# Splitting the weights of each quantum one quantum earlier, across job borders, in a hybrid mLSTM / gated delta rule block

## The chip, the cores and the metric

The kernel runs on one core of a Trainium2 chip. The metric is the device time of one launch in microseconds; for the kernel before, three runs took 1992.89, 1995.98 and 1995.86 us, with a median of 1995.86.

Five engines with an instruction queue each appear below: PE (TensorE, the matrix products), DVE (VectorE, elementwise work from SBUF), ACT (ScalarE, elementwise functions), POOL (GpSimd) and SP (which here issues the loads of weights). PEld is PE's weight load.

## The reference

One layer on 256 tokens of width 2048, in f32, cut to the parts that matter here:

```python
mod = silu(c) @ ada_w + ada_b                 # shift/scale/gate, twice
h = rms_norm(x) * (1 + scale_m) + shift_m
a_q, a_k, a_v, a_o, gates, b_qkv, b_z, gates, merge = split(h @ w_in)
qkv = silu(depthwise_conv5(b_qkv))            # 16 heads of 128: q, k, v
o_b = gated_delta_rule(qkv), both directions  # chunks of 64
h_a = mlstm(a_q, a_k, a_v), both directions   # 4 heads
y_a = (sigmoid(a_o) * rms_norm(h_a)) @ w_branch_a
y_b = (rms_norm(o_b) * silu(b_z)) @ w_branch_b
x = x + gate_m * ((g_a * y_a + g_b * y_b) @ w_out)   # g = sigmoid(merge)
gt, up = split(hf @ w_gate_up)                # hf = modulated rms_norm(x)
x = x + gate_f * ((silu(gt) * up) @ w_down)
out = rms_norm(x)
```

Nearly all the time goes into products of 256 rows with large weight matrices.

## The kernel before

**Products in three parts.** Each f32 weight is split into a high part (`wh`, the value rounded to the fast f32 format of PE) and a low part (`wl`, the rest), and the activations likewise (`hh` and `hl`). A product is the sum of three: high by high, low by high, high by low. The copy to `wh` runs on ACT and the subtraction to `wl` on DVE; both read a 1 MB tile `raw` that SP has loaded from HBM.

**Jobs and quanta.** A *job* is a generator that makes one block of output columns and yields after each *quantum*. `fjob` (L173) makes 128 features by 256 tokens from one raw tile, in 2 quanta of 24 products of 256 columns (L187 to L189). It is used for the heads of the gated delta rule (`b4_0` is head 4, q) and for mLSTM's q and k (`a0_3`). `tjob` (L199) makes 256 tokens by 512 features from four raw tiles or more, in 2 quanta per tile of 12 products of 512 columns (L234 to L236). It is used for v, o, z, the merge gates ma and mb, the branch projections ya and yb, the output projection (also called o, `o_job`), and the FFN's gt, up and d. At the start of a quantum, the halves of its raw tile are split: `fjob` at L182 and L184, `tjob` in `halves` (L207) at L213 and L215. Some t jobs (z0, o0, o3, gt0 and d3) are called with `early` or `by_token`: they split a fixed number of quanta ahead, with some of their instructions in written order.

**Buffers.** `raw`, `wh` and `wl` are tags of one pool with three buffers each, shared by all jobs; a new tile of a tag waits until the oldest one has been read for the last time. Until late in the kernel the tiles of the adaLN product (`ada`) use the `raw` tag as well. That product is done by the DVE, 64 tiles in all, and `raw_tile` (L136), `pump` and `add` spread it between the jobs.

**Order.** The program is a list in Python's order, which a scheduler uses as priority: it may let a ready instruction of an engine pass one that waits, except for those that `order` keeps in program order. `fills` is a list of jobs for which nothing waits soon, and `fill(n)` (L269) runs n quanta of its first job: v0 to v3, mb0, o0, a0_3, ma0, mb1, o1, a1_0 and so on. `stream(h0)` (L879) runs the six b jobs of two heads, then fills; between the quanta the caller places pieces of the recurrences (`gdn_phase1`, `gdn_phase2`). So a job in `fills` may be stopped in the middle and go on after a stream. `invert(g)` runs the DVE's inversion for four heads among fills, after `z_job(g)` was put in front of the fills (L1052). `y_bs` (L1110) runs the four yb jobs, as a fill of the mLSTM part.

**What is put off.** `settle` (L146) runs steps kept in `behind`, such as the SiLU that ends a convolution (L341, `vf`). Each split calls it between the copy and the subtraction.

The jobs start as follows in the profiled execution (us): z0 138, v0 to v3 161 to 234, mb0 259, o0 279, a0_3 300, ma0 306, b4 317, b5 336, b6 375, b7 394, mb1 417, z1 433, o1 466, a1 487, b8 496, b9 518, b10 564, b11 586, ma1 613, z2 624, mb2 662, o2 684, b12 690, b13 709, b14 750, b15 769, a2 800, z3 812, ma2 850, mb3 871, o3 897, a3 927, ma3 958, yb0 996, ya0 1101, gt0 1279, d0 1750. The first 140 us are the adaLN products on PE and the first heads' projections, as their loads arrive.

Of the kernel before, what the change touches and what calls it, by code (L numbers as in the profile page):

```python
# [9 lines left out]
F32 = mybir.dt.float32  # L10
F32R = mybir.dt.float32r
AF = mybir.ActivationFunctionType
ALU = mybir.AluOpType
PSUM = bass.MemoryType.PSUM

P = 128
# [36 lines left out]
def hybrid_block(ctx: ExitStack, tc: tile.TileContext, xr, nfr, crow, pk_d, cst_d, ada2, ada4, win0, winb, wint, wba, wbb, wo, wgu, wd, out, dbg=None):  # L53
# [17 lines left out]
    def order(ins, yes=True):  # L71

        return tc.keep_in_program_order(ins) if yes else ins
# [62 lines left out]
    def raw_tile(shape, name):  # L136

        since[0] += 1
        if since[0] > 2 and asked and room[0][0] is st:
            add()  # L140
        return st.tile(shape, F32, tag="raw", bufs=3, name=name)
# [4 lines left out]
    def settle(keep=0, only=None):  # L146

        now = [f for f in behind if only is None or f.__name__ == only]
        for f in now[: len(now) - keep]:
            behind.remove(f)  # L150
            f()
# [13 lines left out]
    def pump():  # L165
# [3 lines left out]
        if owed[0] and not held[0]:  # L169
            owed[0] -= 1  # L170
            sums()

    def fjob(name, src, done):  # L173

        ps = acc_ps.tile([P, 512], F32, tag="acc", name=f"acc_{name}")
        o = ps[:, :T]
        raw = raw_tile([P, KB, P], f"raw_{name}")
        nc.sync.dma_start(raw, src)
        for k0 in range(0, KB, 8):
            wh = st.tile([P, 8, P], F32R, tag="wh", bufs=3, name=f"wh_{name}_{k0}")  # L180
            wl = st.tile([P, 8, P], F32R, tag="wl", bufs=3, name=f"wl_{name}_{k0}")
            S.activation(wh, raw[:, k0 : k0 + 8], AF.Copy)  # L182
            settle()
            V.tensor_tensor(wl, raw[:, k0 : k0 + 8], wh.bitcast(F32), ALU.subtract)  # L184
            for k in range(8):
                kk = k0 + k
                PE.matmul(o, wh[:, k], woven(hh[:, kk]), start=kk == 0, stop=False)  # L187
                PE.matmul(o, wh[:, k], woven(hl[:, kk]), start=False, stop=False)  # L188
                PE.matmul(o, wl[:, k], woven(hh[:, kk]), start=False, stop=kk == KB - 1)  # L189
            if k0:  # L190
                pump()
                done(o.rearrange("p (c h) -> p h c", h=2))
            yield True
# [3 lines left out]
        return a.rearrange("p (h c) -> p c h", h=n)  # L197

    def tjob(name, chunks, xh, xl, done, early=0, by_token=None, steps=1, parts=((0, slice(0, 512)), (1, slice(0, 512)))):  # L199

        raws = {}

        def halves(u, k0):  # L207
            if u not in raws:
                raws[u] = raw_tile([P, 4, 512], f"raw_{name}_{u}")
                nc.sync.dma_start(raws[u], chunks[u])  # L210
            wh = st.tile([P, 2, 512], F32R, tag="wh", bufs=3, name=f"wh_{name}_{u}_{k0}")
            wl = st.tile([P, 2, 512], F32R, tag="wl", bufs=3, name=f"wl_{name}_{u}_{k0}")
            order(S.activation(wh, raws[u][:, k0 : k0 + 2], AF.Copy), early)  # L213
            settle()
            order(V.tensor_tensor(wl, raws[u][:, k0 : k0 + 2], wh.bitcast(F32), ALU.subtract), early)  # L215
            return wh, wl

        todo = [(u, k0) for u in range(len(chunks)) for k0 in (0, 2)]
        made = []
        for i, q in enumerate(todo[:early]):  # L220
            made.append(halves(*q))
            if steps > 1 or i == early - 1:
                yield True
        ps = [acc_ps.tile([P, 512], F32, tag="acc", name=f"acc_{name}_{t}") for t in range(2)]
        last = 4 * len(chunks) - 1
        if by_token:
            todo = todo[:-2]
        for n, (u, k0) in enumerate(todo):
            wh, wl = made.pop(0) if made else halves(u, k0)
            for k in range(2):  # L230
                kk = 4 * u + k0 + k
                for t in range(2):
                    c = slice(t * P, (t + 1) * P)
                    order(PE.matmul(ps[t], xh[:, kk, c], woven(wh[:, k]), start=kk == 0, stop=False), early and steps > 1)  # L234
                    PE.matmul(ps[t], xl[:, kk, c], woven(wh[:, k]), start=False, stop=False)  # L235
                    PE.matmul(ps[t], xh[:, kk, c], woven(wl[:, k]), start=False, stop=kk == last)  # L236
            if k0:
                pump()
                if u == len(chunks) - 1:
                    done(ps)  # L240
            yield True
            if early and steps > 1:
                if n + early < len(todo):
                    made.append(halves(*todo[n + early]))
                yield True
        if by_token:
            w = [halves(len(chunks) - 1, k0) for k0 in (0, 2)]
            by_token()
            for i, (t, part) in enumerate(parts):
                if i > 1:  # L250
                    ps.append(acc_ps.tile([P, 512], F32, tag="acc", name=f"acc_{name}_{i}"))
                c = slice(t * P, (t + 1) * P)
                o = ps[i][:, : part.stop - part.start]
                for k in range(4):
                    kk = last - 3 + k
                    wh, wl = (woven(a[:, k % 2])[:, part.start // 2 : part.stop // 2] for a in w[k // 2])
                    PE.matmul(o, xh[:, kk, c], wh, start=i == 2 and not k, stop=False)
                    PE.matmul(o, xl[:, kk, c], wh, start=False, stop=False)
                    PE.matmul(o, xh[:, kk, c], wl, start=False, stop=kk == last)
                done(t, ps[i], part)  # L260
                yield True
# [7 lines left out]
    def fill(n=1):  # L269

        while n and fills:
            if next(fills[0], None):
                n -= 1
            else:
                fills.pop(0)
# [97 lines left out]
    def b_job(h, j):  # L373
        return fjob(f"b{h}_{j}", winb[3 * (h - GRP) + j], lambda ps: gdn_conv(h, j, ps))
# [504 lines left out]
    def stream(h0):  # L879

        todo = []

        def piece():

            for q in list(todo):
                q[0] -= 1
                if not q[0]:
                    todo.remove(q)
                    next(heads1[q[1]])

        for h in range(h0, min(h0 + 2, NH_B)):
            for j in range(3):
                for _ in b_job(h, j):
                    piece()
                    yield True
            todo += [[2, h], [4, h]]
        while todo:
            fill(1)
            piece()
            yield True  # L900
        while True:
            fill(1)
            yield True
# [204 lines left out]
            split(mgh[:, b : b + 2], mgl[:, b : b + 2], px.rearrange("p (e t) -> p e t", e=2))  # L1108

    def y_bs():  # L1110
        for g in range(4):
            yield from y_b(g)

    o4s = [o_load(g) for g in range(2)]
    every[0] = owed[0] = 0
# [111 lines left out]
    class Late:  # L1227


        def __init__(self, key):  # L1230
            self.key = key
# [319 lines left out]
```

## Time and profile before

| | |
|---|---|
| runs | 1992.89, 1995.98, 1995.86 us (median 1995.86) |
| profiled execution | 1994.6 us |
| its span | 1992.6 us |
| mean granted PE clock | 0.992 of full speed |
| busy: PE / DVE / ACT | 1943.2 / 1393.9 / 1023.7 us |
| copies L182 (b) and L213 (d): mean | 1056 and 1056 ns |
| subtraction L184 (b): mean | 1216 ns |
| adaLN operation L111: mean, count | 2284 ns, 64 |
| loads raw_b: issue to landing, 1 MB | 5.3 us, median |

A group's row gives line, engine, operation, output and inputs with shapes, and the count; then busy time and the mean duration of one in ns; then how long the engine was idle just before these instructions, and what ended most of that. A row of waits says which instruction's line waited for which: total us, times, longest. A row of a timeline gives start, duration, engine and line; a bracket holds the idle time before. Products overlap: a product of 256 columns lasts 0.28 us in such a row, but the next starts 0.11 us later.

### The profile page before, as it was taken

Reading aid. Unit: us, or ns where it says so; the run is one execution under the profiler, and the core shown is the slowest. Engines: PE = TensorE matmul, PEld = TensorE weight load, DVE = VectorE, ACT = ScalarE, POOL = GpSimd, SP = SyncE. Lnnn points to the kernel's source line nnn. Section 1 sums busy time; section 2 is a strip of 40 time slices with the busy share of each in tenths; the row PEclk is TensorE's granted clock in tenths of the full one; section 3 lists DMA queues with packets and bytes.
Section 4 is the critical chain, followed back from the end, with each engine's and each line's share of the span. In section 5 each row is a group of like instructions: output and inputs, shape, how many; then the busy total and the mean of one; then the engine's idle time right before and its main releaser. Section 6 shows DMA issues by size and latency. Waiting matters only on the chain.

```text
span 1992.6 us, 27027 instructions
## 1 busy us (share of the span) xinstructions
PE 1943.2 (98%) x10386; PEld 1700.4 (85%) x10386; DVE 1393.9 (70%) x2062; ACT 1023.7 (51%) x1541; POOL 116.8 (6%) x211
## 2 busy tenths in 40 slices
PE   8999999999999999999999999999999999999998
PEld 6878789988988899889787888888888888888886
DVE  5778887877878788867576778866666665555554
ACT  3136646765756577655544444554444444444443
POOL 0001210111001101010100000200000000000000
PEclk9999999999989999999999999999999999999999
DMA  9987676655666666587786888466676775555654
GB/s 400 420 336 232 181 245 242 203 183 207 215 197 226 235 235 228 197 283 271 248 300 234 355 298 325 170 252 234 243 263 232 245 262 195 206 199 202 209 195 145
DMA packets 78962, 485.64 MB, mean 244 GB/s; under 512 B 10585, under 2 KB 15969, under 8 KB 24433
## 3 DMA queue, kind: packets, MB, share of 16 engines
q1 hardware_dynamic: 63216, 450.69, 62.4%
q0 software_dynamic: 8160, 17.88, 4.2%
q10 hardware_dynamic: 7458, 15.36, 2.1%
q8 instruction: 81, 1.33, 0.3%
q14 instruction: 47, 0.39, 0.1%
HBM read 467.07 MB, written 16.82 MB: 243 GB/s over the span
## 4 chain that ended last, share of the span: by engine, by line
PE 72%; DVE 12%; DMA 10%; ACT 3%; issue 2%; POOL 0%; ACTq 0%; SPq 0%; DVEq 0%; POOLq 0%
PE acc_gt L234 4%; PE acc_gt L235 4%; PE acc_gt L236 4%; PE acc_up L236 4%; PE acc_up L234 4%; PE acc_up L235 4%; PE acc_d L236 4%; PE acc_d L234 4%; PE acc_d L235 4%; DMA ra<-ada 3%; PE acc_o L236 2%; PE acc_o L234 2%; PE acc_o L235 2%; DMA ada<-ada 2%; PE acc_ya L236 1%
## 5 line engine op out<-in xcount | busy, mean ns | idle before, releaser
L215 DVE TENSOR_TENSOR wl_d<-raw_d,wh_d 128x1024 fp32r<-128x1024 f32 x88 | 107.7, 1224 | 109.2 <-ACT wh_d L213 109.2
L215 DVE TENSOR_TENSOR wl_up<-raw_up,wh_up 128x1024 fp32r<-128x1024 f32 x88 | 107.6, 1224 | 99.9 <-ACT wh_up L213 99.9
L215 DVE TENSOR_TENSOR wl_gt<-raw_gt,wh_gt 128x1024 fp32r<-128x1024 f32 x88 | 108.5, 1233 | 80.0 <-ACT wh_gt L213 80.0
L187 PE MATMUL acc_b<-hh,wh_b 128*128 128x256 f32 x576 | 164.2, 285 | 0.0
L189 PE MATMUL acc_b<-hh,wl_b 128*128 128x256 f32 x576 | 160.2, 278 | 0.1
L188 PE MATMUL acc_b<-hl,wh_b 128*128 128x256 f32 x576 | 159.2, 276 | 0.0
L213 ACT ACTIVATE wh_d<-raw_d 128x1024 fp32r<-128x1024 f32 x88 | 92.9, 1056 | 128.0 <-PE acc_d L235 119.2
L111 DVE SCALAR_TENSOR_TENSOR ada<-ada,crow 128x2048 f32<-128x2048 f32 x64 | 146.2, 2284 | 12.7 <-DMA ada<-ada 12.5
L213 ACT ACTIVATE wh_gt<-raw_gt 128x1024 fp32r<-128x1024 f32 x88 | 92.9, 1056 | 118.6 <-PE acc_gt L235 71.0
L213 ACT ACTIVATE wh_up<-raw_up 128x1024 fp32r<-128x1024 f32 x88 | 92.8, 1055 | 108.1 <-PE acc_up L235 77.1
L234 PE MATMUL acc_gt<-wh_gt,hfh 128*128 128x512 f32 x352 | 135.4, 385 | 0.2 <-ACT hfh L1338 0.2
L235 PE MATMUL acc_gt<-wh_gt,hfl 128*128 128x512 f32 x352 | 134.8, 383 | 0.0
L236 PE MATMUL acc_gt<-wl_gt,hfh 128*128 128x512 f32 x352 | 133.7, 380 | 0.0
L234 PE MATMUL acc_up<-wh_up,hfh 128*128 128x512 f32 x352 | 133.4, 379 | 0.0
L235 PE MATMUL acc_up<-wh_up,hfl 128*128 128x512 f32 x352 | 133.4, 379 | 0.0
L236 PE MATMUL acc_up<-wl_up,hfh 128*128 128x512 f32 x352 | 133.4, 379 | 0.0
L234 PE MATMUL acc_d<-wh_d,ffh 128*128 128x512 f32 x344 | 130.9, 380 | 0.0
L235 PE MATMUL acc_d<-wh_d,ffl 128*128 128x512 f32 x344 | 130.9, 380 | 0.0
L236 PE MATMUL acc_d<-wl_d,ffh 128*128 128x512 f32 x344 | 130.4, 379 | 0.0
L561 PE MATMUL first<-x,raw 128*128 128x256 f32 x512 | 114.5, 382 | 6.9 <-ACT x L555 6.2
L561 PEld LDWEIGHTS first<-x,raw 128*128 128x128 f32 x512 | 96.0, 190 | 25.3 <-ACT x L555 11.8
L189 PEld LDWEIGHTS acc_b<-hh,wl_b 128*128 128x128 f32 x576 | 111.3, 193 | 1.2 <-DVE wl_b L184 1.1
(374 smaller groups left out, 5237.5 us busy)
## 6 DMA issues: line engine op xcount, KB each, us to landing
ada<-ada SPq DMA_DIRECT2D x64, 1024.0 KB, 5.0
raw_gt<-wgu SPq DMA_DIRECT2D x44, 1024.0 KB, 4.9
raw_up<-wgu SPq DMA_DIRECT2D x44, 1024.0 KB, 4.9
raw_d<-wd SPq DMA_DIRECT2D x44, 1024.0 KB, 4.8
raw_b<-winb SPq DMA_DIRECT2D x36, 1024.0 KB, 5.3
ra<-ada SPq DMA_DIRECT2D x32, 1025.0 KB, 15.7
raw<-win SPq DMA_DIRECT2D x16, 1024.0 KB, 14.5
raw_z<-wint SPq DMA_DIRECT2D x16, 1024.0 KB, 5.2
```

The source lines that it names most:

```text
L111: order(V.scalar_tensor_tensor(raw, raw, 1.0, row_c[:, :D], ALU.mult, ALU.mult, accum_out=mod[:, c : c + 1]), room[0][3] > 1)
L187: PE.matmul(o, wh[:, k], woven(hh[:, kk]), start=kk == 0, stop=False)
L188: PE.matmul(o, wh[:, k], woven(hl[:, kk]), start=False, stop=False)
L189: PE.matmul(o, wl[:, k], woven(hh[:, kk]), start=False, stop=kk == KB - 1)
L213: order(S.activation(wh, raws[u][:, k0 : k0 + 2], AF.Copy), early)
L215: order(V.tensor_tensor(wl, raws[u][:, k0 : k0 + 2], wh.bitcast(F32), ALU.subtract), early)
L234: order(PE.matmul(ps[t], xh[:, kk, c], woven(wh[:, k]), start=kk == 0, stop=False), early and steps > 1)
L235: PE.matmul(ps[t], xl[:, kk, c], woven(wh[:, k]), start=False, stop=False)
L236: PE.matmul(ps[t], xh[:, kk, c], woven(wl[:, k]), start=False, stop=kk == last)
L561: PE.matmul(first[o], raw[:, o], x[:, b], start=b == 0 and o % 2 == 0, stop=b == KB - 1 and o % 2 == 1)
```

## The change

A class `Job` wraps the generators. `prime()` runs a job up to a first `yield` that now stands behind its first split, so that a job's load, copy and subtraction come ahead of the products of whatever runs before. `near_end` primes the next job when the present one has a quantum left; it is called in `fill`, for the next fill, and in `stream`, for the next b job or, behind the last, the first fill. Within a job, `tquanta` makes the split of the next quantum ahead of the products of the present one, and `fquanta` makes its second split ahead of its first products. The `settle()` of a split moves ahead of its copy. `y_bs` primes the next yb job ahead of the present one's last quantum. Jobs with `early` or `by_token` stay as they were, and so do the numbers of buffers.

```diff
--- before.py
+++ after.py
@@ -170,18 +170,54 @@
             owed[0] -= 1
             sums()
 
+    class Job:
+
+
+        def __init__(self, gen, quanta):
+            self.gen, self.left, self.primed = gen, quanta, False
+
+        def prime(self):
+            if not self.primed:
+                self.primed = True
+                next(self.gen)
+
+        def __iter__(self):
+            return self
+
+        def __next__(self):
+            self.prime()
+            self.left -= 1
+            return next(self.gen)
+
+    def near_end(job, after):
+
+        if isinstance(job, Job) and job.left == 1 and isinstance(after, Job):
+            after.prime()
+
     def fjob(name, src, done):
-
+        return Job(fquanta(name, src, done), 2)
+
+    def fquanta(name, src, done):
+
+        raw = raw_tile([P, KB, P], f"raw_{name}")
+        nc.sync.dma_start(raw, src)
+
+        def halves(k0):
+            wh = st.tile([P, 8, P], F32R, tag="wh", bufs=3, name=f"wh_{name}_{k0}")
+            wl = st.tile([P, 8, P], F32R, tag="wl", bufs=3, name=f"wl_{name}_{k0}")
+            settle()
+            S.activation(wh, raw[:, k0 : k0 + 8], AF.Copy)
+            V.tensor_tensor(wl, raw[:, k0 : k0 + 8], wh.bitcast(F32), ALU.subtract)
+            return wh, wl
+
+        made = [halves(0)]
+        yield False
         ps = acc_ps.tile([P, 512], F32, tag="acc", name=f"acc_{name}")
         o = ps[:, :T]
-        raw = raw_tile([P, KB, P], f"raw_{name}")
-        nc.sync.dma_start(raw, src)
         for k0 in range(0, KB, 8):
-            wh = st.tile([P, 8, P], F32R, tag="wh", bufs=3, name=f"wh_{name}_{k0}")
-            wl = st.tile([P, 8, P], F32R, tag="wl", bufs=3, name=f"wl_{name}_{k0}")
-            S.activation(wh, raw[:, k0 : k0 + 8], AF.Copy)
-            settle()
-            V.tensor_tensor(wl, raw[:, k0 : k0 + 8], wh.bitcast(F32), ALU.subtract)
+            if not k0:
+                made.append(halves(8))
+            wh, wl = made.pop(0)
             for k in range(8):
                 kk = k0 + k
                 PE.matmul(o, wh[:, k], woven(hh[:, kk]), start=kk == 0, stop=False)
@@ -197,12 +233,17 @@
         return a.rearrange("p (h c) -> p c h", h=n)
 
     def tjob(name, chunks, xh, xl, done, early=0, by_token=None, steps=1, parts=((0, slice(0, 512)), (1, slice(0, 512)))):
+        gen = tquanta(name, chunks, xh, xl, done, early, by_token, steps, parts)
+        return gen if early or by_token else Job(gen, 2 * len(chunks))
+
+    def tquanta(name, chunks, xh, xl, done, early, by_token, steps, parts):
 
 
 
 
 
         raws = {}
+        ahead = not (early or by_token)
 
         def halves(u, k0):
             if u not in raws:
@@ -210,8 +251,11 @@
                 nc.sync.dma_start(raws[u], chunks[u])
             wh = st.tile([P, 2, 512], F32R, tag="wh", bufs=3, name=f"wh_{name}_{u}_{k0}")
             wl = st.tile([P, 2, 512], F32R, tag="wl", bufs=3, name=f"wl_{name}_{u}_{k0}")
+            if ahead:
+                settle()
             order(S.activation(wh, raws[u][:, k0 : k0 + 2], AF.Copy), early)
-            settle()
+            if not ahead:
+                settle()
             order(V.tensor_tensor(wl, raws[u][:, k0 : k0 + 2], wh.bitcast(F32), ALU.subtract), early)
             return wh, wl
 
@@ -221,11 +265,16 @@
             made.append(halves(*q))
             if steps > 1 or i == early - 1:
                 yield True
+        if ahead:
+            made.append(halves(*todo[0]))
+            yield False
         ps = [acc_ps.tile([P, 512], F32, tag="acc", name=f"acc_{name}_{t}") for t in range(2)]
         last = 4 * len(chunks) - 1
         if by_token:
             todo = todo[:-2]
         for n, (u, k0) in enumerate(todo):
+            if ahead and n + 1 < len(todo):
+                made.append(halves(*todo[n + 1]))
             wh, wl = made.pop(0) if made else halves(u, k0)
             for k in range(2):
                 kk = 4 * u + k0 + k
@@ -269,6 +318,7 @@
     def fill(n=1):
 
         while n and fills:
+            near_end(fills[0], fills[1] if len(fills) > 1 else None)
             if next(fills[0], None):
                 n -= 1
             else:
@@ -888,12 +938,16 @@
                     todo.remove(q)
                     next(heads1[q[1]])
 
-        for h in range(h0, min(h0 + 2, NH_B)):
-            for j in range(3):
-                for _ in b_job(h, j):
-                    piece()
-                    yield True
-            todo += [[2, h], [4, h]]
+        jobs = [(h, j, b_job(h, j)) for h in range(h0, min(h0 + 2, NH_B)) for j in range(3)]
+        while jobs:
+            h, j, job = jobs.pop(0)
+            while job.left:
+                near_end(job, jobs[0][2] if jobs else fills[0] if fills else None)
+                next(job)
+                piece()
+                yield True
+            if j == 2:
+                todo += [[2, h], [4, h]]
         while todo:
             fill(1)
             piece()
@@ -1108,8 +1162,14 @@
             split(mgh[:, b : b + 2], mgl[:, b : b + 2], px.rearrange("p (e t) -> p e t", e=2))
 
     def y_bs():
+        after = y_b(0)
         for g in range(4):
-            yield from y_b(g)
+            job, after = after, None
+            while job.left:
+                if job.left == 1 and g < 3:
+                    after = y_b(g + 1)
+                    after.prime()
+                yield next(job)
 
     o4s = [o_load(g) for g in range(2)]
     every[0] = owed[0] = 0
```

## The prediction

> **What bounds the kernel now.** I read first the page's shares and its chain, then the busy time by stretches, then what TensorE (PE) waited for.
>
> ```profile
> span 1992.6 us, 27027 instructions
> PE 1943.2 (98%) x10386; PEld 1700.4 (85%) x10386; DVE 1393.9 (70%) x2062; ACT 1023.7 (51%) x1541; POOL 116.8 (6%) x211
> ...
> PE 72%; DVE 12%; DMA 10%; ACT 3%; issue 2%; POOL 0%; ACTq 0%; SPq 0%; DVEq 0%; POOLq 0%
> ```
>
> PE is busy 1943.2 of 1992.6 us, so whatever a reordering can win lies in 49 us. By stretches (columns: us, busy time of PE, weight load, VectorE (DVE), ScalarE (ACT) and POOL with counts, granted clock, DMA share, GB/s):
>
> ```profile
> 142.00:310.00 168.00, 163.92 (x783) 139.62 (x782) 138.19 (x279) 104.71 (x158) 29.57 (x55) 1.00 0.71 226
> 310.00:425.00 115.00, 113.67 (x887) 107.49 (x886) 92.71 (x174) 85.88 (x175) 10.43 (x21) 1.00 0.62 203
> 425.00:490.00 65.00, 63.49 (x308) 54.48 (x307) 51.96 (x112) 33.13 (x44) 9.94 (x19) 1.00 0.63 209
> 490.00:612.00 122.00, 114.89 (x943) 110.89 (x942) 95.19 (x177) 80.75 (x165) 9.91 (x20) 0.96 0.62 205
> 612.00:690.00 78.00, 74.29 (x349) 62.37 (x349) 62.25 (x128) 45.65 (x67) 10.48 (x20) 1.00 0.69 234
> 690.00:812.00 122.00, 116.05 (x914) 108.72 (x914) 101.98 (x205) 86.59 (x177) 10.34 (x21) 1.00 0.67 225
> 812.00:892.00 80.00, 78.15 (x443) 69.85 (x444) 62.06 (x108) 44.49 (x64) 12.64 (x23) 1.00 0.70 244
> ...
> 1290.00:1992.60 702.60, 692.76 (x3240) 601.50 (x3238) 402.48 (x395) 314.91 (x344) 0.50 (x1) 0.99 0.62 220
> ```
>
> 310–425, 490–612 and 690–812 hold the streams b4–b7, b8–b11 and b12–b15. PE idles 1.3, 7.1 and 6.0 us there, and in 490–612 it also ran below full clock. From 142 to 892 it idles 25.5 us in all. What it waited for (us in total, times, longest):
>
> ```profile
> PE vps L605 <- ACT vf L341: 6.3, 8, 3.1
> ...
> PE acc_mb L236 <- DVE wl_mb L215: 3.1, 3, 1.5
> PE acc_z L234 <- ACT wh_z L213: 2.5, 1, 2.5
> PE acc_z L236 <- DVE wl_z L215: 2.4, 3, 1.5
> PE acc_v L236 <- DVE wl_v L215: 2.4, 3, 1.4
> PE acc_ma L236 <- DVE wl_ma L215: 2.1, 1, 2.1
> PE p L762 <- DVE pt L754: 1.9, 1, 1.9
> PE p L787 <- DVE pt L776: 1.7, 1, 1.7
> ...
> PE acc_o L236 <- DVE wl_o L215: 0.8, 2, 0.5
> ```
>
> The waits on a split (wh, wl) make 13.3 us. That is the most the change's plain meaning, an earlier split, can win; and no product of the b jobs, the ones most rewritten, stands in these rows.
>
> **The change part by part.** Nothing is added or removed: the counts of products, copies, subtractions and DMAs are equal on every engine. About 225 PE, 194 ACT, 276 DVE instructions and 59 of SP's DMA issues stand elsewhere in the order, POOL's none, nearly all between 142 and 892 us. gt, up and d (1290 to the end) keep their order: 0 us.
>
> *1. When a split can start.* It needs a free wh and wl, of which there are three for all jobs together. In the streams the copy already starts on the release:
>
> ```profile
> 378.04 0.28 PE L188 MATMUL acc_b<-hl,wh_b 128*128 128x256 f32 x1
> ...
> 378.25 1.06 ACT L182 ACTIVATE wh_b<-raw_b 128x1024 fp32r<-128x1024 f32 x1
> ...
> 379.63 2.26 DVE L111 SCALAR_TENSOR_TENSOR ada<-ada,crow 128x2048 f32<-128x2048 f32 x1
> ...
> 382.06 1.18 DVE L184 TENSOR_TENSOR wl_b<-raw_b,wh_b 128x1024 fp32r<-128x1024 f32 x1
> ...
> 384.19 0.28 PE L187 MATMUL acc_b<-hh,wh_b 128*128 128x256 f32 x1
> ```
>
> The last product with the old wh is at 378.04, the copy follows 0.21 us later, and the first product with the new one is at 384.19. So "split one quantum sooner" asks for a buffer that isn't there; the copy would stand earlier in ACT's order and wait.
>
> *2. What priming holds.* A t job left in the middle (ma0 during b4, b5; ma1, z2, mb2 and others later) now keeps one split pair all the time that the stream or the z job in front runs, where before it held none. Those in front get two pairs in place of three. Laying out the instructions of both orders on PE at their steps (0.11 us a product of 256 columns, 0.22 of 512), the product time between a buffer's release and its first use falls from a mean of 7.0 to 3.9 us for 59 quanta in b4–b13, and from 6.1 to 3.2 us for the 24 of z1, z2, z3. The steps come from these rows: first and last of the 24 products of a quantum of b4, and one t quantum of 12 (a window with its PE busy time and count):
>
> ```profile
> 316.99 0.36 PE L187 MATMUL acc_b<-hh,wh_b 128*128 128x256 f32 x1
> ...
> 319.64 0.28 PE L189 MATMUL acc_b<-hh,wl_b 128*128 128x256 f32 x1
> ...
> 440.97:443.56 2.59, 2.59 (x13) 2.27 (x12) 0.00 (x0) 1.00 0.91 378
> ```
>
> One quantum is 2.65 + 0.11 = 2.76 us, and 2.59; in a stream pieces of the recurrence bring the typical lead to 3.46, in a z job 2.81. What must fit in:
>
> ```profile
> L182 ACT ACTIVATE wh_b<-raw_b 128x1024 fp32r<-128x1024 f32 x72 | 75.6, 1056 | 35.2 <-PE acc_b L188 20.1 <-DMA raw_b<-winb 3.3 <-PE acc_ma L235 2.5
> ...
> L184 DVE TENSOR_TENSOR wl_b<-raw_b,wh_b 128x1024 fp32r<-128x1024 f32 x72 | 87.4, 1216 | 25.1 <-ACT wh_b L182 25.0
> ...
> L111 DVE SCALAR_TENSOR_TENSOR ada<-ada,crow 128x2048 f32<-128x2048 f32 x64 | 146.2, 2284 | 12.7 <-DMA ada<-ada 12.5
> ...
> L341 ACT ACT_TABLE_LOAD x17 | 21.8, 1283 | 0.3
> ```
>
> Copy plus subtraction is 1.06 + 1.22 = 2.28 us when nothing stands before them. Against 3.46 that leaves 1.2 us, and 0.5 in a z job. One adaLN operation of 2.28 us in front of the subtraction, or a table load of 1.28 us in front of the copy, is more than that. The example shows it: release 378.04 to end of the subtraction 382.06 + 1.18 = 383.24 is 5.2 us. With three buffers it met a lead of 6.2; with two the products stand still for about 1.7.
>
> Floor: the first quanta of b9 and b11 come out with leads of 1.06 and 1.33 us, below 2.28 whatever else runs: 2.28 × 2 − 2.39 = 2.2 us. Ceiling: every turnaround measured in before, set against its new lead, overruns by 10 us in b4–b7 and b13, 6.6 in b8–b11 at the same rate, and 4.5 in z1 and z2: 21 us. But one delay moves everything behind it, and the next copy is in time then; the same static sum for before gives about twice what PE waited. I take **+10**.
>
> *3. Raw tiles.* The 1 MB loads use three buffers as well, which the adaLN tiles share. A held job pins one about half the time, and SP issues in order, so a load waiting for its buffer holds up those behind it. Before, five loads have a lead of a single subtraction, all in 490–624 us; the dearest (start, us, what; then ACT and two windows at half clock):
>
> ```profile
> 542.70 1.13 DVE wl_a L184
> 543.84 6.28 DMA raw_a<-winb
> ...
> 550.20 1.06 ACT L182 ACTIVATE wh_a<-raw_a 128x1024 fp32r<-128x1024 f32 x1 [4.64 <-DMA raw_a<-winb]
> 551.16 0.40 ACT L341 ACTIVATE vf<-cv 128x256 f32<-128x256 f32 x1
> ...
> 551.80:558.10 6.30, 6.30 (x31) 6.30 (x31) 3.72 (x15) 2.83 (x5) 0.00 (x0) 0.50 0.38 159
> 582.30:585.40 3.10, 3.10 (x16) 3.10 (x16) 2.27 (x3) 2.62 (x4) 0.00 (x0) 0.50 0.46 196
> ```
>
> The load waits for the subtraction; behind it wait the copy and, in ACT's order, vf, for which PE waits 3.1 us; then the clock is 0.50 for 6.30 us, which loses half of them, 3.1 more. In after, this stream's loads have three to five quanta of lead, and vf stands before the next copy, not behind it. So the 3.1 + 3.1 there go, and some of the 3.4 (1.7 in the row of L787, half of 3.10 at low clock) at 580: **−8**. But four loads in b5, b13 and b15 now have a lead of one, and seven of two (five before). At the price that five cost here: **+8**. Net 0, bounds −8 and +8.
>
> The Trainium skill ("TensorE: Matmul & The Clock Gate", section on HAM oscillation) lets the clock fall after an idle gap above some 3.4 us. The trace differs: waits of 3.1 and 1.7 us sufficed here. By the page, waits of 1 to 2 us made in step 2 cost only themselves; by the trace, some would cost double.
>
> *4. Subtractions between the inversion's work* (142–310, 425–490, 612–690, 812–892). The order puts wl one step sooner among the DVE's work, where the 13.3 us of split waits lie. Some are in jobs with written-out order (z0) or wait for a buffer, which no order changes. Bounds 0 and −10 (13.3 without z0's share, estimated at 3); I take **−4**, as the DVE stays 80% busy there (138.19 of 168) and something else is late in their place.
>
> *5. y_bs, o, a3, ma3.* Leads between release and use are equal in both orders: 0.
>
> Sum: 10 + 0 − 4 = **+6**. The profiled execution took 1994.6 us (span 1992.6 and 2.0 around it), so about 2000.6; it lies 1.3 below the median of the runs, 1995.86, which gives **2002**.
>
> **Rivals.**
> (a) *Faster.* The relief in 490–612 is real and the freed slack in the streams absorbs the rest: −8 − 4 and step 2 at its floor, +2.2: −10, 1986. For it: the largest single stall is there, and b products never wait today. Against it: the same load leads reappear in b13 and b15, with step 2's two buffers beside them.
> (b) *No change.* Splits were already as early as buffers allow, and delays hide in each other: within 4 us of 1996. For it: 1.3 us of idle PE in 310–425. Against it: the lead there halves. The Trainium skill ("Trainium Kernel Development and Optimization", Best Practices) recommends two buffers; by that, step 2 costs nothing and this rival or (a) holds. The 5.2 us turnaround above speaks against it.
> (c) *Much slower.* The same shortage of pairs, deciding wherever an adaLN operation or a table load meets a two-pair quantum: once such a wait reaches about 1.7 us it also halves the clock. Step 2 at its ceiling 21, raw loads 0 to +8, step 4 at −4: +17 to +25, 2013 to 2021, about 2017. For it: the turnaround at 378; against: PE's delay gives the split its time back.
>
> **How the numbers follow.** Forecast 0.48, (a) 0.22, (b) 0.14, (c) 0.16. What a measurement can tell from no change is 0.2%, 4 us. The forecast's own range is 1997 to 2011 and leaves 0.08 within 4 us; (b) leaves 0.02 faster. Slower 0.40 + 0.16 = 0.56; same 0.08 + 0.12 = 0.20; faster 0.22 + 0.02 = 0.24. The extremes of the steps are 2.2 − 8 − 10 = −16 and 21 + 8 + 0 = +29; I cut the ends that need every term at one side: 1985 to 2018.
>
> **What would show it.** Step 2: PE waits on wh_b and wl_b, absent now, in b4–b13 and on z1–z3, of 0.5 to 2 us; ACT's idle time before L182 put down to L188 growing. Step 3: the 3.1 us wait of vps on vf and the low clock at 551 gone, idle PE in 490–612 near 3 us, more in 690–812. Step 4: the waits on wl_mb, wl_v and wl_ma smaller. 1290 to the end unchanged within 1 us. If no b or z product waits for its split and 310–425 is no longer than before, step 2 is wrong and with it the sign.

## The result, and the profile after

| | before | changed |
|---|---|---|
| median of six runs each | 1994.66 us (1992.89 to 1995.98) | 2003.63 us (2002.08 to 2010.29) |
| ratio to before, 95% interval | | 1.0055 (1.004 to 1.007) |
| profiled execution: span, mean clock | 1992.6 us, 0.992 | 2000.0 us, 0.992 |

The change makes the kernel about half a percent slower: the medians lie 9.0 us apart, and the interval of the ratio leaves out 1. 2002 was forecast, in a range of 1985 to 2018. The page's first lines and its chain, for the changed kernel:

```profile
span 2000.0 us, 27019 instructions
PE 1946.9 (97%) x10386; PEld 1698.8 (85%) x10386; DVE 1394.9 (70%) x2062; ACT 1022.1 (51%) x1541; POOL 116.4 (6%) x211
...
PE 75%; DVE 9%; DMA 9%; ACT 4%; issue 2%; ACTq 0%; POOL 0%; SPq 0%; DVEq 0%; POOLq 0%
```

The work is the same, the span 7.4 us longer. PE's waits in the changed kernel (us in total, times, longest; L209 and L210 are the f job's copy and subtraction now, L256 and L259 the t job's):

```profile
PE acc_b L225 <- DVE wl_b L210: 6.9, 7, 2.9
...
PE vps L655 <- ACT vf L391: 5.3, 6, 2.3
PE acc_z L285 <- DVE wl_z L259: 4.6, 2, 3.1
PE acc_z L283 <- ACT wh_z L256: 4.1, 1, 4.1
PE acc_b L223 <- ACT wh_b L209: 2.6, 4, 1.4
...
PE acc_v L285 <- DVE wl_v L259: 1.2, 2, 0.7
```

The b jobs, whose products did not wait for a split in any row shown of before, now wait 9.5 us for them, and the z jobs 8.7 in place of 4.9. The fills got what the change was for: mb, ma and o are gone from the list, v is halved. By stretches that begin with a job's first product, so that they hold the same work (each difference is taken between two such products in one trace):

| stretch | before | changed |
|---|---|---|
| b4 to mb1 | 99.9 | 101.1 |
| b8 to ma1 | 116.8 | 114.3 |
| b12 to a2 | 110.5 | 120.0 |
| z1 to o1, z2 to mb2 and z3 to ma2, added | 108.4 | 109.5 |
| gt0 to d0 | 470.5 | 470.9 |

b8 to b11 gained, b12 to b15 lost more. One profile has a scatter of its own: in run 1 below PE runs the very products of before in the same order, and its stretches are 99.4, 115.2 and 109.7 us, and 777.8 from b4 to ya0 where before has 784.4. The 9.5 us of b12 to a2 stand clear of that, the 2.5 of b8 to ma1 do not. Windows over these streams in the changed kernel (us, then busy times and counts of PE, PEld, DVE, ACT and POOL, clock, DMA share, GB/s):

```profile
490.00:606.00 116.00, 109.68 (x909) 103.84 (x908) 92.42 (x172) 77.42 (x161) 8.48 (x17) 0.99 0.63 212
...
687.00:820.00 133.00, 120.17 (x916) 109.84 (x915) 105.39 (x206) 90.29 (x187) 11.82 (x23) 0.99 0.60 206
```

In the second, PE idles 12.8 us, where the window 690 to 812 of before had 6.0.

**A wait for lack of a pair.** Timelines of ACT, DVE and PE around b7's first job (start, duration; the bracket is the idle time before and what ended it):

```profile
394.28 1.06 ACT L209 ACTIVATE wh_b<-raw_b 128x1024 fp32r<-128x1024 f32 x1 [1.27 <-PE acc_b L224]
...
395.26 2.29 DVE L111 SCALAR_TENSOR_TENSOR ada<-ada,crow 128x2048 f32<-128x2048 f32 x1 [1.78 <-DMA ada<-ada]
...
397.88 1.22 DVE L210 TENSOR_TENSOR wl_b<-raw_b,wh_b 128x1024 fp32r<-128x1024 f32 x1
...
399.15 0.38 PE L225 MATMUL acc_b<-hh,wl_b 128*128 128x256 f32 x1 [1.00 <-DVE wl_b L210]
```

The copy starts on the release of its buffer, an adaLN operation stands before the subtraction, and the quantum's first products come 3.4 us after the release: the wait for `wl_b` is 1.00 us. With three pairs free, the release would be that of one quantum earlier, 6.9 us before these products, and the split, done 4.9 us after its release, would be in time.

**A wait for lack of a raw tile.** SP's loads while o2 is paused and b14 and b15 run, changed kernel (start, from first to last issue, count):

```profile
730.20 3.26 SPq L251 DMA_DIRECT2D raw_o<-wint  x2
735.34 0.33 SPq L129 DMA_DIRECT2D ada<-ada  x1
739.57 19.83 SPq L203 DMA_DIRECT2D raw_b<-winb  x4
768.11 0.33 SPq L129 DMA_DIRECT2D ada<-ada  x1
775.30 0.33 SPq L203 DMA_DIRECT2D raw_b<-winb  x1
```

The same loads in the kernel before:

```profile
733.16 8.47 SPq L178 DMA_DIRECT2D raw_b<-winb  x3
...
776.64 0.33 SPq L210 DMA_DIRECT2D raw_o<-wint  x1
```

o2's last tile is loaded at 733 in place of 777. Its first half is split at 743, its second not before o2 goes on: it is read for the last time at 798, after 65 us. Two buffers are left to b14, b15 and the adaLN tiles, and each load leaves when one comes free, as the chain of waits of the changed kernel shows:

```profile
782.55 1.23 DVE wl_b L210
783.78 0.02 issue
783.80 6.44 DMA raw_b<-winb
790.24 0.02 issue
790.26 1.07 ACT wh_b L209
791.33 0.02 issue
791.35 1.23 DVE wl_b L210
```

A subtraction ends, its buffer is loaded anew in 6.4 us, copy and subtraction follow: a loop with nothing to hide it. In before, a paused a1 holds a tile in the same way in front of b8 to b11: a1_1 (478 to 539 us) and a1_3 (544 to 607). The changed kernel holds others as well, ma0_2 and mb1_0 (300 to 418, one behind the other) in front of b4 to b7 and o2_1 (671 to 733) in front of b12 and b13; the table shows little loss in b4 to mb1, and b12 to b14 takes 61.9 us where before takes 60.0. So a held tile does not always cost.

### The profile page after: what moved, and what is told of

It reads as the page before. It is cut to its first block, busy times and chain, and to the rows that moved or that the text cites. A ratio compares the mean times of both kernels' runs of the same rounds, so it can differ in the third digit from the quotient of the medians.

```text
span 2000.0 us, 27019 instructions
## 1 busy us (share of the span) xinstructions
PE 1946.9 (97%) x10386; PEld 1698.8 (85%) x10386; DVE 1394.9 (70%) x2062; ACT 1022.1 (51%) x1541; POOL 116.4 (6%) x211
## 4 chain that ended last, share of the span: by engine, by line
PE 75%; DVE 9%; DMA 9%; ACT 4%; issue 2%; ACTq 0%; POOL 0%; SPq 0%; DVEq 0%; POOLq 0%
PE acc_gt L283 4%; PE acc_gt L284 4%; PE acc_gt L285 4%; PE acc_up L283 4%; PE acc_up L284 4%; PE acc_up L285 4%; PE acc_d L284 4%; PE acc_d L285 4%; PE acc_d L283 4%; DMA ada<-ada 3%; DMA ra<-ada 2%; PE acc_o L285 2%; PE first L611 2%; PE acc_o L283 2%; PE acc_o L284 2%
## 5 line engine op out<-in xcount | busy, mean ns | idle before, releaser
L259 DVE TENSOR_TENSOR wl_d<-raw_d,wh_d 128x1024 fp32r<-128x1024 f32 x88 | 107.8, 1225 | 109.1 <-ACT wh_d L256 109.1
L259 DVE TENSOR_TENSOR wl_up<-raw_up,wh_up 128x1024 fp32r<-128x1024 f32 x88 | 107.6, 1225 | 99.6 <-ACT wh_up L256 99.6
L259 DVE TENSOR_TENSOR wl_gt<-raw_gt,wh_gt 128x1024 fp32r<-128x1024 f32 x88 | 108.2, 1229 | 78.9 <-ACT wh_gt L256 78.9
L256 ACT ACTIVATE wh_d<-raw_d 128x1024 fp32r<-128x1024 f32 x88 | 92.9, 1056 | 128.0 <-PE acc_d L284 119.2
L256 ACT ACTIVATE wh_gt<-raw_gt 128x1024 fp32r<-128x1024 f32 x88 | 92.9, 1056 | 118.6 <-PE acc_gt L284 71.0
L256 ACT ACTIVATE wh_up<-raw_up 128x1024 fp32r<-128x1024 f32 x88 | 92.8, 1055 | 108.1 <-PE acc_up L284 77.1
```

## The experiments

Theory R books the loss to raw tiles that paused jobs hold, P to pairs that they hold, O to the new order of splits among the other work. Ratios are to the kernel before, measured with each group of runs. Stretches are from one profile of each.

**1. A pair held, without the change.** While the six b jobs of a stream run, and in each of z1 to z3, an unused `wh` and `wl` tile is allocated, written by POOL and read at the end.

```diff
+        grip()
         for h in range(h0, min(h0 + 2, NH_B)):
...
             todo += [[2, h], [4, h]]
+        let_go()
...
```

(The calls around z1 to z3, and the two functions, are not shown.)

> The kernel before, with one wh and one wl buffer occupied by an unused tile while the b jobs of a stream run and while z1, z2 and z3 run, and nothing else moved. Theory P (pairs: the loss of the change is the pair of halves that a paused t job holds, step 2 of the prediction): slower than before by 6 to 12 us, with waits of products on wh_b, wl_b and wl_z that before does not have. Theory R (raw tiles: the loss is the 1 MB tile that a paused job holds, and the loads of b14 and b15 that come late for it): within 3 us of before, the copies start later but the products hardly wait.

1992.8 us, ratio 0.9999 (0.9988 to 1.001). It does not count against P, as the trace shows that POOL reads each unused tile right after writing it, the first time as follows:

```profile
311.79 0.10 POOL L887 MEMSET grip_wh<- 128x1 f32 x1 [6.69 <-DVE wl_ma L215]
311.95 0.26 POOL L891 COPY grip_out<-grip_wh 128x1 f32<-128x1 f32 x1
```

No pair was held, so this is the kernel before once more, and a measure of how well the same work repeats in a profile: 6.6 us of difference from b4 to ya0. Nearly all of that is the clock: between b4 and ya0 it is at 0.50 for 20.5 us in before and for 6.8 us here.

**2. Splits ahead inside a tile only, first try.**

```diff
-            if ahead and n + 1 < len(todo):
+            if ahead and not k0:
                 made.append(halves(*todo[n + 1]))
```

> The changed kernel, but a t job splits ahead only inside one raw tile: the second half is split ahead of the products of the first, and no split or load of the next tile or the next t job comes ahead. A paused t job then never holds a raw tile, and holds a pair where it is paused in the middle of a tile. The f jobs split ahead as in the change. Theory R: the time from the first product of b12 to that of a2, 110.5 us before and 120.0 after, is 112 or less, that from b8 to ma1, 116.8 before and 114.3 after, stays at 115 or less, and the whole is near 1990, faster than before. Theory P: half of the streams still run on two pairs, the whole is 1998 to 2002.

2008.3 us, ratio 1.0078 (1.0062 to 1.0094). With this edit the t jobs multiply the second half of each raw tile twice and leave out the first, and each split is made in the quantum that needs it. So its t jobs have no lead, and it says little about R; run 6 makes each split in its place.

**3. The kernel before, fills one quantum further.**

```diff
         next(blocks)
-        fill(1)
+        fill(1 if g else 2)
```

> The kernel before with one quantum of the fills more ahead of the first stream, so that every later stream finds the paused job one quantum further: where it was paused in the middle of a raw tile (tile held) it is now paused between two, and the other way round. Theory R: the stretch b8 to ma1 (116.8 us before) gets shorter by 4 to 8 us, and b12 to a2 (110.5) longer by 4 to 8; the whole within 5 us of before. Theory P: in before no paused job holds a pair, so the stretches stay within 2 us.

1992.6 us, ratio 0.9995 (0.9984 to 1.0005). b8 to ma1 103.5 us (116.8 before), b12 to a2 117.9 (110.5): both go the way that R says, the first by more. The stretches do not hold quite the same work: the first has lost 24 products of a1 (2.7 us) and 24 of the recurrences, the second 12 products of o2 (2.6 us). No tile of a1 is held now, but ma0_2 and mb1_0 are in front of b4 to b7, o2_1 (666 to 730) in front of b12 and b13, and o2_3 (734 to 796) in front of b14 and b15. The loss of the second stretch lies all in b12 to b14, 69.0 us in place of 60.0 for the same count of products; b14 to a2 is 48.9 with one quantum less (50.4 before), so there the held tile cost next to nothing. Where the fills stand when a stream begins is worth some ten microseconds in that stream, without any edit to the splits.

**4. The changed kernel with the same shift.** The same edit.

> The changed kernel with the same one quantum more of the fills ahead of the first stream. Theory R: b12 to a2 (120.0 us after) falls to 113 or less, as its paused job now holds no raw tile, and b8 to ma1 (114.3) rises by 2 to 6; the whole 1994 to 2001. Theory P: a paused job holds a pair whether it stands in the middle of a tile or between two, so b12 to a2 stays within 3 us of 120.0 and the whole within 3 us of the changed kernel's 2003.6.

2014.7 us, ratio 1.0106 (1.0089 to 1.0122): in the time a miss for both theories. No fill's tile is held in front of b12 to b15, and b12 to a2 is still 118.5 us, with 12 products of o2 fewer (2.6 us); P's bound for this stretch holds, R's does not. There are waits of 3.6 us for a step of the inversion (R, L772) up to 705.5 and of 3.1 us for wl_b up to 793.2, and 8.5 us lost to half clock between 690 and 900 (one minus the granted clock, summed over windows of 5 us). Held tiles alone do not foretell a kernel's time.

**5. The changed kernel, o2 alone without a held tile.**

```diff
-            if ahead and n + 1 < len(todo):
+            if ahead and n + 1 < len(todo) and not (name == "o2" and k0):
```

> The changed kernel, but the one t job o2 splits ahead only inside a raw tile, so that it holds no tile (and no pair) while b14 and b15 run; all else as changed. Theory R (a raw tile held by a paused job makes the loads of the stream in front late): the time from the first product of b14 to that of a2, 50.4 us before and 58.2 after, falls to 53 or less, the whole to 1995 to 1999. Rival O (the order: splits of the b jobs that stand ahead of other work of ACT and DVE delay the recurrence, wherever the tiles are): it stays at 56 to 60, the whole at 2001 to 2005.

1993.1 us, ratio 0.9987 (0.997 to 1.0005). From its second tile on, o2 multiplies the second half of the tile twice and leaves out the first; the number and shape of its instructions are unchanged. One job of the fills takes back the whole loss. o2_3 is now loaded when o2 goes on:

```profile
781.81 0.33 SPq L251 DMA_DIRECT2D raw_o<-wint  x1
```

The edit takes both tile and pair from the paused o2 (and o2_1 from in front of b12 and b13), so the run alone does not tell them apart. The trace of the changed kernel does: its waits on splits in b14 and b15 all have 6.6 us or more between the release of the buffer and the first product, and the copies start 5.5 us or more after that release, so they did not wait for the pair. b14 to a2 is 53.3 us (58.2 changed, 50.4 before; 53 was R's bound), a2 to ma2 47.5 (52.3 changed), and the whole lies below the 1995 to 1999 that R gave. Its waits still show the other loss:

```profile
PE acc_z L285 <- DVE wl_z L259: 5.8, 3, 3.0
PE acc_b L225 <- DVE wl_b L210: 4.5, 5, 2.8
```

**6, 7, 8. The change in parts.** Run 6: t jobs split the second half of a tile ahead of the first's products, nothing across tiles or t jobs. Run 7: only the f jobs as changed. Run 8: only the t jobs and `y_bs` as changed.

```diff
 # 6
             wh, wl = made.pop(0) if made else halves(u, k0)
+            if ahead and not k0:
+                made.append(halves(*todo[n + 1]))
 # 7
-        return gen if early or by_token else Job(gen, 2 * len(chunks))
+        return gen
-        ahead = not (early or by_token)
+        ahead = False
 # 8, in fquanta
-            if not k0:
-                made.append(halves(8))
-            wh, wl = made.pop(0)
+            wh, wl = halves(k0)
...
```

(Not shown: run 7 also leaves `y_bs` without priming, and run 8 moves the load and the `settle()` of the f jobs back.)

> The changed kernel, with every t job splitting ahead only inside a raw tile: the second half is split ahead of the products of the first, nothing of the next tile or the next t job comes ahead. No paused t job holds a raw tile. The f jobs are as changed. Theory R: b12 to a2 (110.5 us before, 120.0 after) 113 or less, b8 to ma1 (116.8 before, 114.3 after) 115 or less, the whole 1988 to 1996. Rival O: b12 to a2 116 or more, the whole 1998 to 2004.

> The f jobs as changed (splits ahead, the next f job primed), all t jobs and y_bs as before. Theory R: paused t jobs hold raw tiles where they did before, so b12 to a2 stays within 3 us of the 110.5 us before; the whole 1988 to 1997. Rival O: b4 to mb1 (99.9 before, 101.1 after) and b12 to a2 lose as in the change, the whole 1998 to 2004.

> The t jobs and y_bs as changed (splits ahead, the next t job primed), the f jobs as before, with no split ahead of their products. Theory R: o2 and mb1 hold a raw tile in front of the same streams as in the change, so b14 to a2 is 56 us or more and the whole 1998 to 2005. Rival O: b14 to a2 53 or less, the whole 1990 to 1997.

| | us | ratio | b8 to ma1 | b12 to a2 | b14 to a2 |
|---|---|---|---|---|---|
| 6, inside a tile | 2006.1 | 1.0061 (1.0038 to 1.0084) | 116.5 | 114.1 | 53.7 |
| 7, f jobs only | 2010.3 | 1.0077 (1.0051 to 1.0103) | 123.2 | 115.6 | 53.6 |
| 8, t jobs only | 2016.1 | 1.011 (1.0087 to 1.0133) | 115.0 | 121.4 | 50.0 |

All three are slower than either theory had them. For 8 the trace shows more held tiles than in the change: ma0_2 (303 to 362 us), mb1_0 (357 to 426), a1_1 (489 to 552), a1_3 (556 to 622), o2_1 (689 to 752) and o2_3 (752 to 820), one in front of nearly every stream, and it loses most. But b14 to a2, where R had 56 or more for it, is 50.0, as O had it, although o2_3 is held there:

```profile
750.50 1.46 SPq L247 DMA_DIRECT2D raw_o<-wint  x2
```

So b14 to a2 can be sorted by two things, a held tile of o2 and early splits of the b jobs. Neither: 50.4 (before; 49.6 in run 1). The tile alone: 50.0 (run 8). The early splits alone: 53.3 to 53.7 (runs 5, 6 and 7, each with 1.7 us lost to half clock). Both: 58.2 (changed). In these profiles the held tile costs only where the b jobs also split early. Run 4, with early splits and no tile, does not fit: 55.3 us with one quantum less to do, of which 4.4 are lost to half clock.

In 6 and 7 no t job holds a tile through b12 to b15, and both lose all the same, which R does not explain; for 6 neither R's stretch (113 or less) nor O's (116 or more) came. Most of run 6's loss is one stall elsewhere: mb3 to o3 is 34.7 us in place of 26.9. PE idles 6.6 us there, up to 888.5, for a step of the inversion that stands behind an adaLN operation, whose tile took 9.6 us to come:

```profile
875.03 9.59 DMA ada<-ada
...
888.53 0.47 PE p L824
```

The clock is at half for 10.2 us there, from 883.7. The parts do not add: run 8 alone costs more than the whole change, and 6 and 7 no less than it (their intervals overlap with the change's). What the f jobs' early splits can do is in the chain of run 7 (start, duration, what):

```profile
552.32 8.76 DMA raw_b<-winb
561.08 0.02 issue
561.10 0.04 ACTq L209
561.14 0.04 issue
561.18 0.16 ACT wh_b L209
561.34 0.81 issue
562.15 0.37 ACT ev_a L412
562.51 0.31 ACT vf L391
562.83 0.04 issue
562.87 0.48 PE vps L655
```

b10's copy is asked for a job early, while its tile is still on the way, and ACT's order has vf behind it. PE's product into vps waits 4.6 us here, which is the stall at 551 of before, with another job's copy in front. A second one, of 4.8 us at 633, has z2's copy in front of vf. Low clock follows each, 10.2 us from 560.8 and 6.8 from 632.4.

**9, 10, 11. Other numbers of buffers.** In 9 and 10, four raw and two each of wh and wl, in the kernel before and in the changed one; in 11 only two of wh and wl, in the kernel before.

```diff
-            wh = st.tile([P, 8, P], F32R, tag="wh", bufs=3, name=f"wh_{name}_{k0}")
+            wh = st.tile([P, 8, P], F32R, tag="wh", bufs=2, name=f"wh_{name}_{k0}")
...
-        return st.tile(shape, F32, tag="raw", bufs=3, name=name)
+        return st.tile(shape, F32, tag="raw", bufs=4, name=name)
...
```

> The kernel before with four buffers for raw tiles in place of three, and two for wh and wl each in place of three (the same memory). Theory R (the three raw buffers are what is scarce from 142 to 1000 us; a load leaves when its buffer comes free and an engine's order waits for it): the time from the first product of b4 to the first of ya0, 784.4 us before, falls by 5 to 15 us, in spite of the pairs. Rival O (the order of the splits among the other work sets the loss, not the buffers): 784 within 4 us, or longer for the missing pairs. In both, the FFN behind ya0 may lose, as a quantum of 2.59 us must then hold a copy and a subtraction of 2.3 us.

> The changed kernel with the same buffers: four raw, two wh, two wl. Theory R: with a fourth raw tile the tile that a paused job holds no longer starves the streams: b4 to ya0 (792.6 us after) falls by 10 to 20 us and comes within 4 us of before with these buffers. Rival O: it stays 6 us or more above before with these buffers. Theory P (pairs), by which only one pair is left to the stream in front of a job that holds one: it is slower than the changed kernel by 15 us or more.

> The kernel before with two buffers for wh and wl each in place of three, raw tiles as before. After the run with a pair held, theory P gives 0 to 5 us from b4 to ya0 (784.4 us before), with the b and z jobs on two pairs and the fills too. Its difference to the run with four raw buffers is what the fourth raw buffer is worth: by theory R 8 us or more.

| | us | ratio | b4 to ya0 |
|---|---|---|---|
| 9, before, raw 4, pairs 2 | 2073.3 | 1.0398 (1.0376 to 1.0419) | 816.6 |
| 10, changed, raw 4, pairs 2 | 2089.8 | 1.0483 (1.0457 to 1.0508) | 833.5 |
| 11, before, raw 3, pairs 2 | 2062.5 | 1.0362 (1.0339 to 1.0386) | 819.3 |

Against R as it was put: the fourth raw tile is worth 2.7 us from b4 to ya0 (8 or more expected), less than the 6.6 by which the same work differed in run 1. The third pair is worth 34.9 there (819.3 against 784.4), far over the 0 to 5 expected after run 1. The changed kernel takes 833.5 us on two pairs and 792.6 on three, in spite of the fourth raw tile: P's bound of 15 is passed, R's fall of 10 to 20 did not come, and it stays 16.9 us above run 9, as P and O have it. So a kernel with two pairs all the time loses much; a pair that is missing only at times is not measured by it. Four raw tiles together with three pairs were not tried, so what a fourth tile is worth by itself stays open.

**12. No tile of a1 held, splits as before.**

```diff
         next(blocks)
-        fill(1)
+        fill((1, 2, 0, 1)[g])
```

> The kernel before, with one quantum of the fills more ahead of the streams b8 to b11 and one less ahead of b12 to b15, so that a1 is not paused in the middle of a job while b8, b9 and then b10, b11 run, and the other streams find the fills as before. No split moves ahead of anything. Theory R: the raw tiles a1_1 and a1_3 are no longer held for some 60 us each, b8 to ma1 (116.8 us before, 103.5 with every stream shifted) falls to 103 to 109, b4 to mb1 (99.9) and b12 to a2 (110.5) stay within 2 us, and the whole is 8 to 14 us faster than before, 1980 to 1987. Rivals O and P: no split is ordered in another way and no pair is held or freed, so the whole is within 4 us of before.

1988.0 us, ratio 0.9974 (0.9962 to 0.9985): faster than both kernels, by 5.3 us (3.0 to 7.6) where R expected 8 to 14 and the rivals less than 4. b8 to ma1 is 101.8 us, but one quantum of a1 has moved out of it. From o1 to b12, which holds the same work, it is 215.8 us against 224.3 before and 221.5 in run 1. b12 to a2 is unchanged at 110.5. The stream's window:

```profile
487.00:600.00 113.00, 110.04 (x943) 106.21 (x942) 95.98 (x175) 80.06 (x161) 7.63 (x16) 1.00 0.72 244
```

The same count of products (in nearly the same mix) as in the window 490 to 612 of before, in 113 us instead of 122, at full clock, with the DMA at 244 GB/s instead of 205. PE idles 3.0 us where it idled 7.1.

## Why the prediction was right, and where it was not

**The time** was forecast at 2002 and came out at 2003.6; profile against profile it was +6 and came out at +7.4. That is closer than its terms deserve.

**Step 1**, a copy already starts on the release, so a split can't come sooner: right. Nothing in the changed trace starts earlier than its buffer allows, and waits on wh_b and wl_b appear where there were none.

**Step 2**, the pair that a paused t job holds, +10. The mechanism is there as described, the row at 399 with its adaLN operation most plainly. ACT's idle time before its copies tells the same (before: L213 here, L182 in the prediction; changed: L256 and L209):

```profile
L213 ACT ACTIVATE wh_z<-raw_z 128x1024 fp32r<-128x1024 f32 x32 | 33.2, 1053 | 24.3 <-PE acc_z L235 12.2 <-DMA raw_z<-wint 8.1 <-PE acc_mb L235 3.1
...
L256 ACT ACTIVATE wh_z<-raw_z 128x1024 fp32r<-128x1024 f32 x32 | 33.5, 1054 | 34.1 <-PE acc_z L284 29.9 <-DVE wl_z L259 1.5 <-DMA raw_z<-wint 1.4
L209 ACT ACTIVATE wh_b<-raw_b 128x1024 fp32r<-128x1024 f32 x72 | 75.5, 1055 | 43.6 <-PE acc_b L224 26.1 <-DMA raw_b<-winb 6.3 <-DVE mod L114 3.3
```

The part that waits for a release grew from 12.2 to 29.9 us in the z jobs and from 20.1 to 26.1 in the b jobs. Sorting PE's waits on splits between 300 and 960 us by the time from the buffer's release to the first product (while a job holds a pair, the release of two quanta back), those with a lead under 4.4 us come to 8.3 us: 1.00, 0.77, 0.60 and 2.85 in b7 to b10, 3.06 in z2. In before no waiting quantum has a lead under 5.0. Two of them are not the pair's alone: the copies of the 0.77 and the 2.85 start 2.6 and 1.0 us after the release. Run 11 shows that the third pair is needed. How much of this change's loss the pair made is read from the waits; the run that was to isolate it, the first, held nothing.

**Step 3**, raw tiles, taken at 0 (-8 and +8), is the mis-sized term. The relief in b8 to b11 was smaller, if it came: b8 to ma1 is 2.5 us shorter, 0.9 against run 1, with a wait of 2.9 us at 581 on a subtraction behind a late adaLN tile (step 2's two pairs beside it). The loss was named for b5, b13 and b15 by the leads of their loads; what decided was o2, whose tile o2_3 stood held in front of b14 and b15 while these split early, and run 5 takes the whole loss away with it. So the step is nearer to +8 than to 0. (Its 3.4 us at 580 are 3.3 by the two terms given, which changes nothing.) Run 5 keeps step 2's waits (the two rows above make 10.3 us) and is no slower than before, so gains of about that size stand against them: those of step 4, and the waits on the inversion and the recurrences (the rows of p, pa, pb and pc), which are 6.2 us in before and 1.6 in the changed kernel. The prediction has no term for the latter. That the sum came out within 2 us is luck in part: +8, not 0, here, and gains beyond the -4.

**Step 4**, earlier subtractions among the inversion's work, -4. The waits of mb, v, ma and o make 8.4 us in the rows of before and 1.2 in those of the changed kernel's list above. This is more than was taken, and within the bound of 10. z1 to z3 gave about half of it back, 8.7 us against 4.9.

**Step 5**, no change elsewhere: gt0 to d0 0.4 us longer, yb0 to ya0 2.0 longer and a3 to yb0 2.3 shorter in the one profile of each; run 1, with the work of before, has 2.2 and 1.0 shorter there.

**The marks.** The wait of vps at 551 was to go: it is down to 1.4 us, at 553.8, and half clock follows it as before, for a shorter time. PE's idle time near 3 us in b8 to b11 was wrong, it is 6.3; more of it in b12 to b15 was right. Rival (b) is out, by the waits and by the interval. Rival (c)'s reading of the clock, half speed once a wait reaches about 1.7 us, does not hold in before itself: the waits of 1.91 us up to 501.0, 2.06 up to 654.9 and 2.51 up to 811.9 were not followed by a lower clock. Rival (a) did not come: even without o2's tile the change is no faster than before (0.9987, with 1 in the interval).

**Open.** Why the t jobs' half of the change costs more by itself than the whole (run 8) and the f jobs' half no less (run 7), why a held o2_1 goes with 69.0 and 71.5 us from b12 to b14 in runs 3 and 8 but with 61.9 in the changed kernel, and the shift's cost in run 4: the waits are seen, in another place each time, but no single cause was isolated. The moved `settle()` was not tried by itself.

## What to carry to other kernels

Before splitting or loading ahead, ask what the step needs that is not free yet: a buffer that is released only by the work in front makes the earlier instruction wait in its engine's order, and hold up what is behind it. A job that is paused with a scarce buffer in hand can starve the work in front, though it need not, as runs 3 and 8 show; look at which tiles are loaded long before their last read, and try the pause where it holds none. Here one quantum of the fills, run a stream earlier, won 5 us, where the whole change cost 9. And compare a profile with a second one of the same program first: here two of them differed by 6.6 us in a stretch of 784.

## What the runs showed of the hardware that was not expected

How long PE must idle for its clock to fall is not fixed in these traces (times are those at which a wait ends). 1.72 us at 580.7 in the kernel before was followed by 0.50. In the changed kernel, 1.41 us at 553.8 was followed by a lower clock as well, 2.85 us at 581.1 and 3.06 us at 639.5 were not:

```profile
556.00:560.00 4.00, 4.00 (x13) 2.21 (x12) 2.30 (x7) 1.57 (x3) 0.00 (x0) 0.62 0.29 102
...
582.00:586.00 4.00, 4.00 (x38) 4.00 (x37) 3.05 (x4) 2.17 (x5) 0.00 (x0) 1.00 1.01 420
...
640.00:644.00 4.00, 3.86 (x18) 3.06 (x17) 3.79 (x10) 1.06 (x1) 0.00 (x0) 1.00 0.78 262
...
821.00:825.00 4.00, 4.00 (x11) 3.10 (x10) 0.58 (x1) 0.26 (x1) 0.51 (x1) 0.50 0.59 178
```

The last row follows a wait of 4.13 us at 819.2. In run 5 the same two waits, 2.75 us at 586.0 and 2.98 at 645.2, were both followed by a lower clock (0.57 over 587 to 591, 0.59 over 646 to 649.5). A wait of 1.4 to 3 us may cost its own length, or more than a microsecond on top (4 us at 0.62 lose 1.5), and two profiles of such kernels can differ by several microseconds for that alone, as before and run 1 do.

The traces also show what the length of a wait leaves out. Within each profile the periods of half clock begin at whole multiples of 3.41 us from each other (in before at 551.28, 582.00 and 971.12 us, 9 and 114 such steps apart), and each but the last lasts one step or several. What tells more is how much of a wait falls into one step: of the steps that begin at full clock between 300 and 960 us, in before, the changed kernel and runs 1, 3 to 8 and 12, each with over 2.0 us of idle PE is followed by half clock and none with under 1.2; in between both occur. The wait of 2.85 us that ended at 581.1 lies across the end of a step at 579.5 (1.2 and 1.6 us), the one of 2.98 us in run 5 within a single step.
